# Attention keys and latent queries in DRAM, by head and then row

## The chip, the cores and the metric

The kernel runs on one core of one Trainium2 chip. The metric is device time in microseconds of one execution. A core has TensorE (PE; its weight loads are listed as PEld), VectorE (DVE), ScalarE (ACT), GpSimd (POOL) and SyncE (SP), and 16 DMA engines. Every DMA of this kernel is issued by SyncE, in the order of its one instruction stream.

## What is computed

Two network blocks of two layers each, batch 1, 512 tokens, width 1024, all in float32. The first block mixes sliding-window attention, retention and gated linear attention. The second block also carries 256 context tokens; its even layer has windowed attention and a latent attention of 8 heads, its odd layer grouped and differential attention. Cut to the part in which the change lies, the even layer is:

```
qa, ka, va, cq, ckv, kpe = split_cols(t @ w_in, EVEN_SIZES)
qb  = rms_norm_2(cq, q_norm) @ w_uq           # 8 heads x (64 + 32)
kvb = rms_norm_2(ckv, kv_norm) @ w_ukv        # 8 heads x (64 keys + 64 values)
qb  = [qb[..., :64], rope(qb[..., 64:])]
kb  = [kvb[..., :64], rope(kpe)]
kb_all = concatenate([kb_context, kb])        # 256 + 512 keys
ob  = softmax(qb @ kb_all.T / sqrt(96)) @ vb_all
```

## The kernel before

Activations lie with features on the 128 partitions and tokens along the row. Products are kept near float32 by splitting each operand into a high and a low part and making three products: weights come into `wr`, ScalarE rounds them to `wh`, GpSimd or VectorE makes the rest `wl` (`weights`, L417 to L422, L398, L400). Three `wr` buffers and two of `wh` and `wl` take turns.

Queries, keys and values of each attention are projected first, written to scratch in DRAM (`put`, L816), and read back head by head (`get`, L819). A projected tile has 128 partitions: two heads of 64 rows, or four heads of 32 rows where a rotation handles the two halves of a head apart. The tiles wait in `rp`, nine buffers of the work pool that many steps share; a buffer is free again when its put has landed.

The scratch tensors of keys are `rk` and `ak` (first block), `eka` (even, windowed), `ekn` (even, latent), `okc` and `okd` (odd layer). Each is laid out as [high or low, 64 rows, heads, tokens]. The latent queries without position, `qn` (in DRAM `eqnc` for the context and `eqnm` for the 512 tokens), are laid out as [128, 8 heads, tokens]: rows 0 to 63 high parts, rows 64 to 127 low parts. So in a put of two heads the destination steps over heads first and over rows second, and the two steps can't be joined.

`even_project` makes three generators: `window` (keys, queries and values of the windowed part), `latent`, and the scratch. `latent` normalizes the key latent, then per pair of heads makes one product, splits it into two `rp` tiles and puts both into `ekn` (8 puts); values go to `evb` in 8 puts (4 for the context); the shared rotated key to `ekp`; then the query latent, four products of two heads each and 8 puts into `qn`; then the rotated queries to `qp`. `weave` interleaves generators in proportion to the numbers given to it, and the tile scheduler sets each engine's order from priorities. For the 256 context tokens `latent` is woven into the first steps of the first block's second layer; for the 512 tokens it is woven into `even_window`, the windowed attention, whose blocks it shares PSUM, `rp` and SyncE's queue with. `even_latent` then reads per head `ekn` (four gets of 64 rows), `qn`, `qp` (two gets) and `evb`.

Of the kernel before, what the change touches and what calls it, by code (L numbers as in the profile page):

```python
# [12 lines left out]
F32R = mybir.dt.float32r  # L13
# [11 lines left out]
S = 512  # L25
# [3 lines left out]
TK = S + CL  # L29
# [170 lines left out]
class Net:  # L200
# [627 lines left out]
    def k_put(self, scr, pieces, h0, c0, T, n=4):  # L828

        for xi, parts in enumerate(pieces):  # L830
            for hl, t in enumerate(parts):
                dst = scr[hl, xi * 32:xi * 32 + 32, h0:h0 + n, c0:c0 + T]
                self.put(dst.rearrange("r h t -> h r t"), t)

    def k_put_both(self, scr, parts, c0, T):
        for hl, t in enumerate(parts):
            for xi in range(2):
                dst = scr[hl, xi * 32:xi * 32 + 32, 0:2, c0:c0 + T]
                self.put(dst.rearrange("r h t -> h r t"), t[xi * 64:xi * 64 + 64])

    def k_get(self, at, scr, h, c0, T):

        out = []
        for hl in range(2):
            t = at("k", [128, T], F32R)
            for d in range(2):
                self.get(t[d * 64:d * 64 + 64], scr[hl, :, h, c0:c0 + T])
            out.append(t)
        return out

# [392 lines left out]
    def layer1(self, l, h, ready):  # L1243

        nc, I = self.nc, self.I

        def fm(i):
            return ready.pop(i) if i in ready else self.dense(I["w_in"][l, i].rearrange("p k c -> p (k c)"), h, S, tag="d")

        ob = self.oy1(S)  # L1250
        og, orr = [ob[:, 2], ob[:, 3]], [ob[:, 0], ob[:, 1]]
        rq, rk = self.scr([128, 4, S], f"rq{l}"), self.scr([2, 64, 4, S], f"rk{l}")
        aq, ak = self.scr([128, 8, S], f"aq{l}"), self.scr([2, 64, 2, S], f"ak{l}")
        rv, av = self.scr([128, NT, 4, 128], f"rv{l}"), self.scr([128, NT, 2, 128], f"av{l}")
        gates = self.scr([128, KD, S], f"gate{l}")

        def values(v, n, dst):
            hl = self.rp([128, n, 2, 64], F32R)
            src = v.rearrange("p (h d) -> p h d", d=64)
            self.split_ps(src, hl[:, :, 0, :], hl[:, :, 1, :])  # L1260
            self.put(dst, hl.rearrange("p h a d -> p h (a d)"))

        def project1():
            tab = self.load_angles(self.rtab)
            self.q_put(rq, self.rope(partial(fm, 2), partial(fm, 3), tab, S), 0)
            yield
            self.k_put(rk, self.rope(partial(fm, 4), partial(fm, 5), tab, S), 0, 0, S)
            yield
            for t, v in enumerate(self.dense_tok(I["w_tok_b"][l], h, S, 384, 2)):
                values(v[:, 0:256], 4, rv[:, t])  # L1270
                values(v[:, 256:384], 2, av[:, t])
            yield

        late = 2

        def project2():
            tab = self.load_angles(self.atab)
            self.k_put_both(ak, self.rope_both(fm(6), tab, S), 0, S)
            yield
            for g in range(2):  # L1280
                self.q_put(aq, self.rope(partial(fm, 7 + 2 * g), partial(fm, 8 + 2 * g), tab, S, 0.125), 4 * g)
                yield
            yield from gate_units(range(done, 8 - late))

        def gate_units(units):
            for i in units:
                self.put(gates[:, (6, 7, 4, 5, 0, 1, 2, 3)[i], :], self.silu2(fm(11 + i), S))
                yield

        q, k = (self.tl(self.c1, [128, S], F32, "q", 2) for _ in range(2))  # L1290
        nc.scalar.activation(q, fm(0), AF.Copy, scale=32 ** -0.5)
        yield
        nc.scalar.copy(k, fm(1))
        yield
        p1 = project1()
        done = len(ready)
        self.steps(gate_units(range(done)))
        gv, ga = [], []
        for v in self.dense_tok(I["w_tok_a"][l], h, S, 272, 3):
            gv.append(self.vsplit(v[:, 0:256], 4))  # L1300
            t = self.sm([128, 16])
            nc.scalar.copy(t, v[:, 256:272])
            ga.append(t)
        if l == 0:
            self.setup1()
        gt = self.bank([16, S])
        for t in range(NT):
            nc.tensor.transpose(gt[:, t * 128:t * 128 + 128], ga[t], self.ident)
        gaT = self.pg([16, S])
        nc.scalar.copy(gaT, gt)  # L1310
        yield
        with self.phase("gla") as ph:
            at = self.area(ph, "r", k=2, q=2, v=1)
            self.weave((self.gla(q, k, gv, gaT, l, og, ph), (31.2, 26)[l], 0),
                       (self.chain(p1, self.woven((project2(), (6.6, 24.2)[l], (-200, 0)[l]), (self.retention(at, rq, rk, rv, orr), 16, (300, 45)[l]))), 30, (30, 0)[l]))
        self.headnorm(og, self.gla_gain[:, l:l + 1])
        self.headnorm(orr)
        self.steps(gate_units(range(8 - late, 8)))
        oa = self.oy1(S)
        h = self.new_h(S)  # L1320

        def gated(ks):
            for k in ks:
                g = self.rp([128, S])
                nc.sync.dma_start(g, gates[:, k, :])
                src = oa[:, k, :] if k < 4 else ob[:, k - 4, :]
                nc.vector.scalar_tensor_tensor(src, src, 0.5, g, op0=ALU.mult, op1=ALU.mult)
                self.split(src, h[0][:, k, :], h[1][:, k, :], 1.0, "dve" if k in [1, 3, 5, 7] else "pool")

        gated((6, 7, 4, 5))  # L1330
        y = self.open_y()
        self.stage(low=3)
        with self.phase("win") as ph:
            at = self.area(ph, "w", k=4, q=6, v=2, p=10)
            self.weave((self.window1(at, aq, ak, av, self.sink1[:, l * 8:l * 8 + 8], oa), (26.4, 8)[l], 0),
                       (self.out_head(I["w_out"][l], h, S, y, range(4, 8)), (8, 5.6)[l], 0))
        gated(range(4))
        return h, y, range(4, 8)
# [48 lines left out]
    def setup2(self):  # L1387
        nc, I = self.nc, self.I
        self.cp = self.common
        t = self.pg([128, 384])  # L1390
# [16 lines left out]
        self.lam = self.cp.tile([128, 1], F32, name="lam")  # L1407
        nc.vector.tensor_sub(self.lam, sm[:, 0:1], sm[:, 1:2])
        nc.vector.tensor_scalar(self.lam, self.lam, LAM_INIT, None, op0=ALU.add)
        self.eka = self.scr([2, 64, 2, TK], "eka")  # L1410
        self.eva = self.scr([128, TK // 128, 2, 128], "eva")
        self.ekn = self.scr([2, 64, 8, TK], "ekn")
        self.ekp = self.scr([2, 32, TK], "ekp")
        self.evb = self.scr([128, TK // 128, 8, 128], "evb")
        self.okc = self.scr([2, 64, 2, TK], "okc")
        self.okd = self.scr([2, 64, 8, TK], "okd")
        self.ovc = self.scr([128, TK // 128, 2, 128], "ovc")
        self.ovd = self.scr([128, TK // 128, 2, 4, 128], "ovd")

# [31 lines left out]
    def even_project(self, h, T, c0, rope, pool):  # L1451

        nc, I = self.nc, self.I
        tag = "m" if rope else "c"
        W = I["ev_w_in"]
        fm = lambda i: self.dense(W[i].rearrange("p k c -> p (k c)"), h, T, tag="d")
        sc = dict(q=self.scr([128, 8, T], "eq" + tag), qn=self.scr([128, 8, T], "eqn" + tag),
                  qp=self.scr([64, 8, T], "eqp" + tag))

        def window():  # L1460
# [9 lines left out]
        def latent():  # L1470
# [3 lines left out]
            for i in range(4):  # L1474
                w = slice(i * 128, i * 128 + 128)
                ps = self.three(self.bank([128, T], "d"), [(hi[:, w], lo[:, w])], [ck])
                parts = self.rp([128, T], F32R), self.rp([128, T])
                self.split_ps(ps, *parts)
                for hl, p in enumerate(parts):
                    self.put(self.ekn[hl, :, 2 * i:2 * i + 2, c0:c0 + T].rearrange("r h t -> h r t"), p)  # L1480
            yield
            for t in range(T // 128):
                tok = slice(t * 128, t * 128 + 128)
# [29 lines left out]
            def up(hi, lo, i):  # L1513
                w = [slice(i * 256 + k * 128, i * 256 + k * 128 + 128) for k in range(2)]
                return self.three(self.bank([128, T], "d"), [(hi[:, s], lo[:, s]) for s in w], cq)
# [3 lines left out]
            for i in range(4):  # L1519
                parts = self.rp([128, T], F32R), self.rp([128, T])  # L1520
                self.split_ps(up(*w, i), *parts, sb)
                for hl, p in enumerate(parts):
                    self.put(sc["qn"][hl * 64:hl * 64 + 64, 2 * i:2 * i + 2, :].rearrange("r h t -> h r t"), p)
            yield
            w = self.weights(src[:, 1024:], 512)
            self.q_put(sc["qp"], self.rope(partial(up, *w, 0), partial(up, *w, 1), tab, T, sb), 0, 8, 16)
# [67 lines left out]
    def even_latent(self, at, sc, T, K, o):  # L1594
# [7 lines left out]

        def block(hd):
            kh, kl = self.k_get(at, self.ekn, hd, 0, K)
            qn = self.q_get(at, sc["qn"], hd, T)
            qp = at("q", [128, T], F32R)
            for d in range(2):
                self.get(qp[d * 64:d * 64 + 64], sc["qp"][:, hd, :])
            v = at("v", [128, K // 128, 128], F32R)
# [398 lines left out]
```

## Time and profile before

| | us |
|---|---|
| median of 3 runs (lowest, highest) | 2809.75 (2808.07, 2816.77) |
| the profiled execution, its time | 2816.5 |
| its span, first to last instruction | 2814.7 |

The profile is of one execution; the time of that execution is 1.8 us above its span. The mean granted TensorE clock over the span is 0.916 of full speed. The span is one chain of stages on one core; what a stage waits for is read from the rows of that stage. In rows in order of time a bracket gives the idle time of the engine before the instruction and what ended it. Times in the rows are us from the start of the span.

### The profile page before, as it was taken

The numbers are of one execution on the slowest core, as the hardware profiler recorded it, in microseconds if no ns is written. First come the engines' busy times: TensorE is split into PE (matmuls) and PEld (weight loads), VectorE is DVE, ScalarE is ACT, GpSimd is POOL, SyncE is SP. The second block draws the span as 40 slices with busy tenths as digits, with TensorE's granted clock in tenths as the row PEclk, the third lists the DMA queues.
The fourth block names the chain that finished last, engine by engine and source line by source line (L and its number), as shares of the span: only waits on it lengthen the run. The fifth ranks groups of instructions, "written<-read, shape, count | busy, mean of one in ns | idle before, by whom it ended". The sixth has DMA issues, their size and how long they took to land. (4 is left out here: it accounts for less than half of the span.)

```text
span 2814.7 us, 35280 instructions
## 1 busy us (share of the span) xinstructions
PE 2440.7 (87%) x12956; PEld 1984.9 (71%) x12956; DVE 1260.6 (45%) x2101; ACT 1178.0 (42%) x2219; POOL 1060.7 (38%) x754
## 2 busy tenths in 40 slices
PE   6978887778878886568999899999988989799997
PEld 4766666566666665447998887777776777688886
DVE  3655356244646644355452631222555777421212
ACT  3434364343537634346554532222344656332222
POOL 2435234334533541113444732323552222443334
PEclk9988898888979987779999999999988999899998
DMA  7364553335334553325653545454344353333332
GB/s 244 117 209 158 181 183 137 119 130 174 116 109 139 194 193 119 119 97 143 185 159 134 181 141 172 150 172 137 126 155 155 102 162 104 115 100 97 94 97 75
DMA packets 170816, 400.56 MB, mean 142 GB/s; under 512 B 19378, under 2 KB 60820, under 8 KB 167316
## 3 DMA queue, kind: packets, MB, share of 16 engines
q1 hardware_dynamic: 170644, 398.31, 43.3%
q8 instruction: 103, 1.69, 0.2%
q14 instruction: 69, 0.57, 0.1%
HBM read 339.85 MB, written 58.39 MB: 141 GB/s over the span
## 5 line engine op out<-in xcount | busy, mean ns | idle before, releaser
L398 POOL TENSOR_TENSOR wl<-wr,wh 128x1024 fp32r<-128x1024 f32 (+3 forms) x245 | 537.7, 2196 | 889.4 <-ACT wh L422 463.9
L422 ACT CAST wh<-wr 128x1024 fp32r<-128x1024 f32 (+3 forms) x367 | 353.9, 964 | 706.3 <-PE d L389 277.8
L389 PE MATMUL d<-hh,wh 128*128 128x512 f32 x960 | 398.7, 415 | 19.2 <-ACT hh L556 7.8
L389 PE MATMUL d<-hl,wh 128*128 128x512 f32 x960 | 393.4, 410 | 0.9 <-DVE hl L557 0.9
L389 PE MATMUL d<-hh,wl 128*128 128x512 f32 x960 | 261.4, 401 | 0.0
L400 DVE SCALAR_TENSOR_TENSOR wl<-wr,wh 128x1024 fp32r<-128x1024 f32 (+3 forms) x122 | 147.6, 1210 | 230.9 <-PE d L389 97.1
L389 PEld LDWEIGHTS d<-hh,wh 128*128 128x128 f32 x960 | 190.3, 198 | 61.3 <-ACT hh L556 8.4
L389 PEld LDWEIGHTS d<-hl,wh 128*128 128x128 f32 x960 | 189.8, 198 | 40.2 <-issue 2.9
L389 PEld LDWEIGHTS d<-hh,wl 128*128 128x128 f32 x960 | 184.3, 193 | 39.9 <-issue 1.6
L389 PE MATMUL b<-hh,wh 128*128 128x512 f32 x416 | 164.8, 396 | 0.0
L389 PE MATMUL b<-hl,wh 128*128 128x512 f32 x416 | 163.6, 393 | 0.0
L400 DVE SCALAR_TENSOR_TENSOR pg<-b,pg 128x512 fp32r<-128x512 f32 (+1 forms) x208 | 137.5, 667 | 54.9 <-ACT pg L404 50.4
L404 ACT CAST pg<-b 128x512 fp32r<-128x512 f32 (+1 forms) x208 | 117.5, 573 | 63.6 <-PE b L909 52.9
L882 DVE TENSOR_REDUCE sm<-s 128x1 f32<-128x768 f32 (+3 forms) x144 | 120.8, 847 | 30.8 <-PE s L389 29.8
L389 PE MATMUL d<-hc,wh 128*128 128x256 f32 x656 | 107.6, 315 | 22.5 <-DVE rp L400 11.4
L963 DVE SCALAR_TENSOR_TENSOR rp<-rp,d 128x512 f32<-128x512 f32 (+1 forms) x77 | 46.8, 608 | 167.8 <-ACT rp L962 167.6
L389 PE MATMUL d<-hid,wh 128*128 128x512 f32 (+1 forms) x528 | 115.6, 363 | 1.7 <-POOL hid L398 1.5
L1770 DVE SCALAR_TENSOR_TENSOR rp<-rp,b 128x512 f32<-128x512 f32 (+1 forms) x64 | 38.1, 595 | 175.0 <-PE b L389 174.3
L389 PEld LDWEIGHTS d<-hc,wh 128*128 128x128 f32 x656 | 97.3, 217 | 26.5 <-ACT wh L422 11.7
L389 PE MATMUL b<-hid,wh 128*128 128x512 f32 (+1 forms) x528 | 112.4, 361 | 0.0
L389 PE MATMUL b<-hh,wl 128*128 128x512 f32 x416 | 104.2, 390 | 0.0
L389 PEld LDWEIGHTS d<-hid,wh 128*128 128x128 f32 x528 | 90.7, 192 | 17.3 <-POOL hid L398 2.7
(419 smaller groups left out, 5062.6 us busy)
## 6 DMA issues: line engine op xcount, KB each, us to landing
wr<-in_ffn_w_in SPq DMA_DIRECT2D x132, 512.0 KB
mr<-in_ada_w SPq DMA_DIRECT2D x96, 512.0 KB
wr<-in_ffn_w_out SPq DMA_DIRECT2D x48, 512.0 KB
x<-x SPq DMA_DIRECT2D x20, 1024.0 KB
wr<-in_w_in SPq DMA_DIRECT2D x38, 512.0 KB
mr<-in_w_mod SPq DMA_DIRECT2D x32, 512.0 KB
wr<-in_ev_w_in SPq DMA_DIRECT2D x20, 512.0 KB
wr<-in_ffn_w_out SPq DMA_DIRECT2D x24, 384.0 KB
```

The costliest lines, as they stand in the source:

```text
L389: self.nc.tensor.matmul(out, lhsT, rhs, start=start, stop=stop)
L398: self.nc.gpsimd.tensor_sub(out, src, hi)
L400: self.nc.vector.scalar_tensor_tensor(out, src, scale, hi, op0=ALU.mult, op1=ALU.subtract)
L404: self.nc.scalar.copy(hi, src)
L422: nc.scalar.copy(hi[:, :n], raw[:, :n])
L882: nc.vector.reduce_max(c, s, axis=AX.X, negate=True)
L963: nc.vector.scalar_tensor_tensor(t, t, 1.0, ps, op0=ALU.add, op1=ALU.mult)
L1770: nc.vector.scalar_tensor_tensor(g, g, 0.5, pu, op0=ALU.mult, op1=ALU.mult)
```

## The change

The key scratch tensors get the layout [high or low, heads, 64 rows, tokens], and `qn` becomes [2, 8 heads, 64 rows, tokens]. `k_put`, `k_put_both` and `k_get` index accordingly. The puts of `ekn` and `qn` name their destination as one run of 128 rows, two heads of 64. A head's `qn` now lies in two places, high and low, so that its read becomes two gets of 64 rows.

```
--- before.py
+++ after.py
@@ -829,14 +829,12 @@
 
         for xi, parts in enumerate(pieces):
             for hl, t in enumerate(parts):
-                dst = scr[hl, xi * 32:xi * 32 + 32, h0:h0 + n, c0:c0 + T]
-                self.put(dst.rearrange("r h t -> h r t"), t)
+                self.put(scr[hl, h0:h0 + n, xi * 32:xi * 32 + 32, c0:c0 + T], t)
 
     def k_put_both(self, scr, parts, c0, T):
         for hl, t in enumerate(parts):
             for xi in range(2):
-                dst = scr[hl, xi * 32:xi * 32 + 32, 0:2, c0:c0 + T]
-                self.put(dst.rearrange("r h t -> h r t"), t[xi * 64:xi * 64 + 64])
+                self.put(scr[hl, 0:2, xi * 32:xi * 32 + 32, c0:c0 + T], t[xi * 64:xi * 64 + 64])
 
     def k_get(self, at, scr, h, c0, T):
 
@@ -844,7 +842,7 @@
         for hl in range(2):
             t = at("k", [128, T], F32R)
             for d in range(2):
-                self.get(t[d * 64:d * 64 + 64], scr[hl, :, h, c0:c0 + T])
+                self.get(t[d * 64:d * 64 + 64], scr[hl, h, :, c0:c0 + T])
             out.append(t)
         return out
 
@@ -1249,8 +1247,8 @@
 
         ob = self.oy1(S)
         og, orr = [ob[:, 2], ob[:, 3]], [ob[:, 0], ob[:, 1]]
-        rq, rk = self.scr([128, 4, S], f"rq{l}"), self.scr([2, 64, 4, S], f"rk{l}")
-        aq, ak = self.scr([128, 8, S], f"aq{l}"), self.scr([2, 64, 2, S], f"ak{l}")
+        rq, rk = self.scr([128, 4, S], f"rq{l}"), self.scr([2, 4, 64, S], f"rk{l}")
+        aq, ak = self.scr([128, 8, S], f"aq{l}"), self.scr([2, 2, 64, S], f"ak{l}")
         rv, av = self.scr([128, NT, 4, 128], f"rv{l}"), self.scr([128, NT, 2, 128], f"av{l}")
         gates = self.scr([128, KD, S], f"gate{l}")
 
@@ -1407,13 +1405,13 @@
         self.lam = self.cp.tile([128, 1], F32, name="lam")
         nc.vector.tensor_sub(self.lam, sm[:, 0:1], sm[:, 1:2])
         nc.vector.tensor_scalar(self.lam, self.lam, LAM_INIT, None, op0=ALU.add)
-        self.eka = self.scr([2, 64, 2, TK], "eka")
+        self.eka = self.scr([2, 2, 64, TK], "eka")
         self.eva = self.scr([128, TK // 128, 2, 128], "eva")
-        self.ekn = self.scr([2, 64, 8, TK], "ekn")
+        self.ekn = self.scr([2, 8, 64, TK], "ekn")
         self.ekp = self.scr([2, 32, TK], "ekp")
         self.evb = self.scr([128, TK // 128, 8, 128], "evb")
-        self.okc = self.scr([2, 64, 2, TK], "okc")
-        self.okd = self.scr([2, 64, 8, TK], "okd")
+        self.okc = self.scr([2, 2, 64, TK], "okc")
+        self.okd = self.scr([2, 8, 64, TK], "okd")
         self.ovc = self.scr([128, TK // 128, 2, 128], "ovc")
         self.ovd = self.scr([128, TK // 128, 2, 4, 128], "ovd")
 
@@ -1454,7 +1452,7 @@
         tag = "m" if rope else "c"
         W = I["ev_w_in"]
         fm = lambda i: self.dense(W[i].rearrange("p k c -> p (k c)"), h, T, tag="d")
-        sc = dict(q=self.scr([128, 8, T], "eq" + tag), qn=self.scr([128, 8, T], "eqn" + tag),
+        sc = dict(q=self.scr([128, 8, T], "eq" + tag), qn=self.scr([2, 8, 64, T], "eqn" + tag),
                   qp=self.scr([64, 8, T], "eqp" + tag))
 
         def window():
@@ -1477,7 +1475,7 @@
                 parts = self.rp([128, T], F32R), self.rp([128, T])
                 self.split_ps(ps, *parts)
                 for hl, p in enumerate(parts):
-                    self.put(self.ekn[hl, :, 2 * i:2 * i + 2, c0:c0 + T].rearrange("r h t -> h r t"), p)
+                    self.put(self.ekn[hl, 2 * i:2 * i + 2, :, c0:c0 + T].rearrange("h r t -> (h r) t"), p)
             yield
             for t in range(T // 128):
                 tok = slice(t * 128, t * 128 + 128)
@@ -1520,7 +1518,7 @@
                 parts = self.rp([128, T], F32R), self.rp([128, T])
                 self.split_ps(up(*w, i), *parts, sb)
                 for hl, p in enumerate(parts):
-                    self.put(sc["qn"][hl * 64:hl * 64 + 64, 2 * i:2 * i + 2, :].rearrange("r h t -> h r t"), p)
+                    self.put(sc["qn"][hl, 2 * i:2 * i + 2].rearrange("h r t -> (h r) t"), p)
             yield
             w = self.weights(src[:, 1024:], 512)
             self.q_put(sc["qp"], self.rope(partial(up, *w, 0), partial(up, *w, 1), tab, T, sb), 0, 8, 16)
@@ -1602,8 +1600,9 @@
 
         def block(hd):
             kh, kl = self.k_get(at, self.ekn, hd, 0, K)
-            qn = self.q_get(at, sc["qn"], hd, T)
-            qp = at("q", [128, T], F32R)
+            qn, qp = at("q", [128, T], F32R), at("q", [128, T], F32R)
+            for d in range(2):
+                self.get(qn[d * 64:d * 64 + 64], sc["qn"][d, hd])
             for d in range(2):
                 self.get(qp[d * 64:d * 64 + 64], sc["qp"][:, hd, :])
             v = at("v", [128, K // 128, 128], F32R)
```

The first place is SyncE's stream where the context's latent queries are put; `eqnc` is their DRAM tensor, `rp` the tiles in SBUF, `wr` a weight load. This is one piece of the difference.

```order
-L816 DMA eqnc<-rp_4588 2x64x256
-L816 DMA eqnc<-rp_4589 2x64x256
-L816 DMA eqnc<-rp_4601 2x64x256
-L816 DMA eqnc<-rp_4602 2x64x256
+L816 DMA eqnc<-rp_4588 128x256
+L816 DMA eqnc<-rp_4589 128x256
+L816 DMA eqnc<-rp_4601 128x256
+L816 DMA eqnc<-rp_4602 128x256
 L417 DMA wr_4758<-in_w_tok_a 128x544
```

The order is the same; the destination of each put reads 128 rows where it read two times 64.

The second place is the last two key puts of the 512 tokens and what SyncE issues behind them: queries of the window (`eq`), latent values (`evb`), and keys of the window's second group (`ek` from `eka`). Before:

```order
L816 DMA ekn<-rp_9538 2x64x512
L816 DMA ekn<-rp_9539 2x64x512
L819 DMA eq_9879<-eqm 128x512
L819 DMA eq_9881<-eqm 128x512
L819 DMA eq_9883<-eqm 128x512
L816 DMA evb<-rp_9665 128x512
L819 DMA ek_9871<-eka 64x768
L816 DMA evb<-rp_9669 128x512
L819 DMA ek_9871<-eka 64x768
L816 DMA evb<-rp_9677 128x512
L816 DMA evb<-rp_9681 128x512
L816 DMA evb<-rp_9689 128x512
```

And with the change:

```order
L816 DMA ekn<-rp_9546 128x512
L816 DMA ekn<-rp_9547 128x512
L819 DMA eq_9887<-eqm 128x512
L819 DMA eq_9889<-eqm 128x512
L819 DMA eq_9891<-eqm 128x512
L816 DMA evb<-rp_9673 128x512
L819 DMA ek_9879<-eka 64x768
L816 DMA evb<-rp_9677 128x512
L819 DMA ek_9879<-eka 64x768
L816 DMA evb<-rp_9685 128x512
L816 DMA evb<-rp_9689 128x512
L816 DMA evb<-rp_9697 128x512
```

No DMA has moved past another; the two puts changed their shape.

The third place is the reads of the first two heads of the 512 tokens in `even_latent`. Before:

```order
L819 DMA ek_10656<-ekn 64x768 x2
L819 DMA ek_10659<-ekn 64x768 x2
L819 DMA eq_10662<-eqnm 128x512
L819 DMA eq_10664<-eqpm 64x512 x2
L819 DMA ev_10667<-evb 128x6x128
L819 DMA ek_10713<-ekn 64x768 x2
L819 DMA ek_10716<-ekn 64x768 x2
L819 DMA eq_10719<-eqnm 128x512
L819 DMA eq_10721<-eqpm 64x512 x2
L819 DMA ev_10724<-evb 128x6x128
```

And with the change:

```order
L819 DMA ek_10664<-ekn 64x768 x2
L819 DMA ek_10667<-ekn 64x768 x2
L819 DMA eq_10670<-eqnm 64x512 x2
L819 DMA eq_10671<-eqpm 64x512 x2
L819 DMA ev_10676<-evb 128x6x128
L819 DMA ek_10722<-ekn 64x768 x2
L819 DMA ek_10725<-ekn 64x768 x2
L819 DMA eq_10728<-eqnm 64x512 x2
L819 DMA eq_10729<-eqpm 64x512 x2
L819 DMA ev_10734<-evb 128x6x128
```

Each head has one more get, the second half of `qn`, ahead of its `qp`. In the two loops of `even_latent` the 16 added gets shift some weight loads and value reads by a few places; elsewhere SyncE's order, and that of the other engines, is the one of before.

The 8 key puts and 8 query puts for the context and as many for the 512 tokens, 32 in all, are the only ones whose shape changes. The puts of `okd` and `rk` stay four heads of 32 rows, those of `ak`, `eka` and `okc` two heads of 32 rows; only the distance between heads and rows in DRAM is another. The key reads stay 64 rows, which now lie next to each other.

## Rows read from the trace of the kernel before

**Rows 1.** The page: the span, and TensorE with its share.

```profile
span 2814.7 us, 35280 instructions
...
PE 2440.7 (87%) x12956; PEld 1984.9 (71%) x12956; DVE 1260.6 (45%) x2101; ACT 1178.0 (42%) x2219; POOL 1060.7 (38%) x754
```

**Rows 2.** By tile, SyncE issues: ns min/median/max, first and last start us.

```profile
L819 SPq DMA_DIRECT2D ek<-ekn x32: 444/564/1392, 1248.2 to 1419.6; - x32
...
L816 SPq DMA_DIRECT2D ekn<-rp x16: 495/2688/5262, 516.0 to 1129.2; - x16
...
L816 SPq DMA_DIRECT2D eqnm<-rp x8: 485/4487/5209, 1198.8 to 1224.2; - x8
...
L816 SPq DMA_DIRECT2D gate<-rp x16: 319/358/1974, 87.9 to 826.7; - x16
```

**Rows 3.** Stretches: length, busy PE, PEld, DVE, ACT, POOL; PEclk, DMA share, GB/s.

```profile
519.00:548.00 29.00, 14.28 (x81) 12.89 (x79) 3.24 (x6) 6.94 (x13) 5.28 (x3) 0.80 0.35 121
575.00:596.00 21.00, 8.92 (x31) 6.04 (x30) 2.83 (x5) 5.12 (x12) 2.37 (x1) 0.59 0.60 212
1110.00:1134.00 24.00, 9.54 (x46) 6.51 (x44) 8.26 (x22) 8.32 (x22) 0.74 (x1) 0.72 0.13 52
1116.00:1153.00 37.00, 4.53 (x18) 2.71 (x18) 6.23 (x14) 5.41 (x13) 0.00 (x0) 0.56 0.34 123
1153.00:1160.00 7.00, 6.92 (x25) 5.27 (x25) 1.08 (x3) 1.46 (x4) 0.53 (x2) 0.65 0.54 160
1223.00:1249.00 26.00, 6.16 (x27) 2.68 (x26) 5.51 (x11) 5.84 (x15) 1.47 (x2) 0.50 0.43 147
```

**Rows 4.** In order of time, SyncE, 1085 to 1165 us: start, length, DMAs.

```profile
1104.02 30.46 SPq L816 DMA_DIRECT2D ekn<-rp  x8
...
1147.83 2.95 SPq L816 DMA_DIRECT2D evb<-rp  x5
```

**Rows 5.** Who waited for whom, 1085 to 1160 us: total, times, longest.

```profile
ACT rp L404 <- DMA ekn<-rp: 22.4, 6, 4.8
```

**Rows 6.** In order of time, TensorE; in brackets idle before, and releaser.

```profile
1123.09 1.22 PE L389 MATMUL d<-wh,lat 128*128 128x512 f32 x2 [3.71 <-DVE rp L400]
...
1129.22 0.66 PE L942 MATMUL b<-ident,pg 128*128 128x128 f32 x2 [4.49 <-DVE sm L894]
1152.61 0.55 PE L389 MATMUL s<-ek,eq 128*128 128x256 f32 x1 [22.73 <-DMA ek<-eka]
```

**Rows 7.** In order of time, SyncE then TensorE, 1198 to 1250 us.

```profile
1198.79 30.37 SPq L816 DMA_DIRECT2D eqnm<-rp  x8
...
1228.43 1.65 PE L389 MATMUL d<-pg,ev 128*128 128x512 f32 x2 [4.84 <-ACT pg L404]
1238.45 0.79 PE L389 MATMUL d<-pg,ev 128*128 128x512 f32 x1 [8.38 <-ACT pg L404]
...
1248.53 1.01 PE L389 MATMUL b<-mod_sel,ms 128*128 128x2 f32 x4 [6.57 <-ACT pg L944]
```

**Rows 8.** Who waited for whom, 1180 to 1270 us.

```profile
ACT rp L503 <- DMA eqnm<-rp: 13.5, 3, 4.8
...
ACT rp L406 <- DMA eqnm<-rp: 3.8, 1, 3.8
```

**Rows 9.** In order of time, SyncE, ScalarE and TensorE, 516 to 592 us.

```profile
517.16 17.07 SPq L816 DMA_DIRECT2D ekn<-rp  x7
...
546.32 1.04 ACT L422 CAST wh<-wr 128x1024 fp32r<-128x1024 f32 x1 [9.10 <-DMA wr<-in_ev_w_uq]
...
579.44 1.04 ACT L422 CAST wh<-wr 128x1024 fp32r<-128x1024 f32 x1 [8.75 <-DMA wr<-in_w_in]
...
548.01 1.01 PE L389 MATMUL b<-blk,rp 128*128 128x1 f32 x4 [9.14 <-ACT rp L503]
...
582.34 0.38 PE L1308 MATMUL b<-ident,sm 128*16 128x128 f32 x1 [7.02 <-ACT sm L1302]
...
589.91 0.38 PE L1308 MATMUL b<-ident,sm 128*16 128x128 f32 x1 [5.05 <-ACT sm L1302]
```

More of the change, by code (lines that the diff above doesn't have):

```diff
@@ L831, in k_put @@
             for hl, t in enumerate(parts):
-                dst = scr[hl, xi * 32:xi * 32 + 32, h0:h0 + n, c0:c0 + T]
-                self.put(dst.rearrange("r h t -> h r t"), t)
+                self.put(scr[hl, h0:h0 + n, xi * 32:xi * 32 + 32, c0:c0 + T], t)
     def k_put_both(self, scr, parts, c0, T):
@@ L837, in k_put_both @@
             for xi in range(2):
-                dst = scr[hl, xi * 32:xi * 32 + 32, 0:2, c0:c0 + T]
-                self.put(dst.rearrange("r h t -> h r t"), t[xi * 64:xi * 64 + 64])
+                self.put(scr[hl, 0:2, xi * 32:xi * 32 + 32, c0:c0 + T], t[xi * 64:xi * 64 + 64])
     def k_get(self, at, scr, h, c0, T):
@@ L846, in k_get @@
             for d in range(2):
-                self.get(t[d * 64:d * 64 + 64], scr[hl, :, h, c0:c0 + T])
+                self.get(t[d * 64:d * 64 + 64], scr[hl, h, :, c0:c0 + T])
             out.append(t)
@@ L1251, in layer1 @@
         og, orr = [ob[:, 2], ob[:, 3]], [ob[:, 0], ob[:, 1]]
-        rq, rk = self.scr([128, 4, S], f"rq{l}"), self.scr([2, 64, 4, S], f"rk{l}")
-        aq, ak = self.scr([128, 8, S], f"aq{l}"), self.scr([2, 64, 2, S], f"ak{l}")
+        rq, rk = self.scr([128, 4, S], f"rq{l}"), self.scr([2, 4, 64, S], f"rk{l}")
+        aq, ak = self.scr([128, 8, S], f"aq{l}"), self.scr([2, 2, 64, S], f"ak{l}")
         rv, av = self.scr([128, NT, 4, 128], f"rv{l}"), self.scr([128, NT, 2, 128], f"av{l}")
@@ L1409, in setup2 @@
         nc.vector.tensor_scalar(self.lam, self.lam, LAM_INIT, None, op0=ALU.add)
-        self.eka = self.scr([2, 64, 2, TK], "eka")
+        self.eka = self.scr([2, 2, 64, TK], "eka")
         self.eva = self.scr([128, TK // 128, 2, 128], "eva")
-        self.ekn = self.scr([2, 64, 8, TK], "ekn")
+        self.ekn = self.scr([2, 8, 64, TK], "ekn")
         self.ekp = self.scr([2, 32, TK], "ekp")
         self.evb = self.scr([128, TK // 128, 8, 128], "evb")
-        self.okc = self.scr([2, 64, 2, TK], "okc")
-        self.okd = self.scr([2, 64, 8, TK], "okd")
+        self.okc = self.scr([2, 2, 64, TK], "okc")
+        self.okd = self.scr([2, 8, 64, TK], "okd")
         self.ovc = self.scr([128, TK // 128, 2, 128], "ovc")
@@ L1456, in even_project @@
         fm = lambda i: self.dense(W[i].rearrange("p k c -> p (k c)"), h, T, tag="d")
-        sc = dict(q=self.scr([128, 8, T], "eq" + tag), qn=self.scr([128, 8, T], "eqn" + tag),
+        sc = dict(q=self.scr([128, 8, T], "eq" + tag), qn=self.scr([2, 8, 64, T], "eqn" + tag),
                   qp=self.scr([64, 8, T], "eqp" + tag))
@@ L1479, in latent @@
                 for hl, p in enumerate(parts):
-                    self.put(self.ekn[hl, :, 2 * i:2 * i + 2, c0:c0 + T].rearrange("r h t -> h r t"), p)
+                    self.put(self.ekn[hl, 2 * i:2 * i + 2, :, c0:c0 + T].rearrange("h r t -> (h r) t"), p)
             yield
@@ L1522, in latent @@
                 for hl, p in enumerate(parts):
-                    self.put(sc["qn"][hl * 64:hl * 64 + 64, 2 * i:2 * i + 2, :].rearrange("r h t -> h r t"), p)
+                    self.put(sc["qn"][hl, 2 * i:2 * i + 2].rearrange("h r t -> (h r) t"), p)
             yield
@@ L1604, in block @@
             kh, kl = self.k_get(at, self.ekn, hd, 0, K)
-            qn = self.q_get(at, sc["qn"], hd, T)
-            qp = at("q", [128, T], F32R)
+            qn, qp = at("q", [128, T], F32R), at("q", [128, T], F32R)
+            for d in range(2):
+                self.get(qn[d * 64:d * 64 + 64], sc["qn"][d, hd])
             for d in range(2):
```

## Prediction

> **What bounds the kernel now.** TensorE is busy 87% of the span [rows 1], so most stages are TensorE's, and a change that only moves DMA data is worth something only where TensorE stands still because of it. I therefore looked for the changed transfers first, by tile: what SyncE spends on issuing them. A put of 256 KB whose rows are one run (`gate<-rp`, 128 rows of 512) takes SyncE 358 ns in the median. The puts of `ekn` take 2688 ns in the median and up to 5262, those of `eqnm` 4487 and up to 5209, though the latter are as large as `gate<-rp` [rows 2]. An issue that long is not the instruction's own work; SyncE is held back by something that is full.
>
> The windows say what. While the 512 tokens' key puts run, from 1110 to 1134 us, the 16 DMA engines are busy 0.13 of the time, at 52 GB/s [rows 3]. 0.13 times 16 is 2.1 engines. The reader is to see a core with 14 idle DMA engines whose SyncE can't get rid of its puts: eight puts of 256 KB are 2.1 MB, and at 52 GB/s that is 40 us. In order of time this is just what happens: the eight puts begin at 1104.02, take SyncE 30.46 us to issue, and the run of value puts behind them starts only at 1147.83 [rows 4].
>
> The Trainium skill gives a reason ("DMA: Bandwidth & Descriptors", on why a DMA increments its semaphore by 16, the paragraph on how many engines): a DMA is spread over as many engines, up to 16, as divide the size of the slowest dimension of both sides. For a destination of two heads by 64 rows that is 2. The trace agrees with its 0.13.
>
> Who suffers: ScalarE waits 22.4 us in 6 waits for `rp` buffers that `ekn` puts still hold [rows 5], and its stream stands meanwhile, so that VectorE and then TensorE run dry. TensorE idles 3.71, 4.49 and at last 22.73 us, the last for `ek`, the window's keys of its second group, whose gets are behind those puts and the value puts in SyncE's stream [rows 6]. Over 1116 to 1153 it is busy 4.53 of 37 us, at a granted clock of 0.56; there is nothing else that fills the hole.
>
> The same shape comes three more times. The `eqnm` puts hold SyncE from 1198.79 for 30.37 us, and TensorE idles 4.84, 8.38 and 6.57 us [rows 7], behind ScalarE's 13.5 and 3.8 us of waiting for them [rows 8]. For the context the puts are half as long: `ekn` holds SyncE 17.07 us from 517.16, weight loads queue behind it, ScalarE waits 9.10 us for one, TensorE 9.14 for ScalarE; then `eqnc`, where ScalarE waits 8.75 us for a weight load and TensorE stands for 7.02 and 5.05 us [rows 9].
>
> **The change part by part.**
>
> The 32 puts of `ekn` and `qn` get 128 rows as their outer dimension on both sides. I price one like `gate<-rp`: 0.36 us of SyncE, and data on all engines. If 16 engines do what 2 did, 43.8 us (1104.02 to 1147.83) become 5.5 us for eight puts, less than the 6 or so us that producing the tiles takes; the hold is gone. Stretch by stretch:
>
> - 1116 to 1153. The last `ek` get has to wait for the value puts ahead of it, and these for splits that stood behind the held `rp` buffers. Without the hold I let the three idle stretches of 30.9 us [rows 6] shrink to one last wait of 4 us, the latency of the get and the rest of the splits: 27 us saved. Bounds: TensorE's idle time is 32.5 us; a quarter of it may come back, so 20 to 32.
> - 1223 to 1249. TensorE is idle 19.8 us [rows 7]. The four rotated query puts (`eqpm`, eight heads by 16 rows) keep their shape and still run there, so 3 us stay: 17 saved, 12 to 22 (above 19.8 since the work there runs at a clock of 0.50 [rows 3], the lower level of 1.2 GHz, and would mostly run at the upper).
> - 519 to 548. Idle 29.00 - 14.28 = 14.7 us [rows 3]; weight loads still have to land, so 13 saved, 7 to 17 with the clock of 0.80.
> - 575 to 596. Idle 21.00 - 8.92 = 12.1 us at a clock of 0.59. Three loads still have to come in a row after the puts: 9 saved, 4 to 15.
>
> Sum of the four: 66 us. What follows each stretch is TensorE's (1153 to 1160: 6.92 busy of 7.00 [rows 3]), so an earlier start is an earlier end.
>
> The clock comes back late after a stall: 0.65 in 1153 to 1160 though TensorE is full [rows 3]. At the upper level those 6.9 us would be 4.5. I don't add this, it is in the upper bounds.
>
> The reads of `qn` become two gets of 64 rows: 16 more DMAs. The trace has a get of 64 rows: `ek<-ekn`, 564 ns of SyncE [rows 2], so 9.0 us of SyncE in all. They lie in the two loops of `even_latent`, where a head's reads go out while TensorE works on the head before. On the path is the first head's only: 0.6 us per loop, 1 us in all. Lower bound 0, upper bound 9.0 if every one delays its head. The Trainium skill speaks against this part ("DMA: Bandwidth & Descriptors", rules for kernel authors: don't cut a transfer into partition halves, one of 128 partitions is better). By that rule alone the loss would be some part of the 9.0 us; I keep 1.
>
> The other layouts (`rk`, `ak`, `eka`, `okc`, `okd`): their puts keep two or four heads as outer dimension, so what holds them back stays; their gets and those of `ekn` read 64 rows that are now neighbours, with the same rows and bytes. I cost this at nothing; what hides it is that the reads of one head run under the work on another. A gain or loss of 2 us either way is in the range.
>
> 66 - 1 = 65 us less. The profiled execution took 2816.5 us (span 2814.7), so the sum gives 2751.5 for it; that execution was 6.75 us above the median of the three, 2809.75. In terms of the median: 2744.75, say **2745**.
>
> **The rivals.**
>
> *The holes close only in part.* Where the hold goes, the next thing in line may be nearly as late: at 1152.61 the get of `ek` also stands behind eight value puts, and in the context's stretch behind weight loads which need a free `wr` buffer. For it: TensorE is idle 13% of the time even away from here. Against: between the puts SyncE has nothing else to do for long, and DMA is nearly empty. If half of each lower bound were all that came (20 + 12 + 7 + 4 = 43, halved 22), the time is 2788; I let this case reach from 2772 to 2801.
>
> *Nothing changes.* It could be that two engines are used not because of the two heads, but because of the rows' distance in DRAM or of `rp` as the source; then 128 rows in one run fill the same two. For it: nothing in the rows names the cause. Against: `gate<-rp` comes from `rp` too, with 128 rows, and takes 358 ns. The time would be 2810 plus 1 for the gets, 2811.
>
> *Slower.* The two key reads per head and the two halves of `qn` now come out of one dense block each, and a dense block may be read slower than rows far apart; with the added gets each head of `even_latent` then starts late. It decides from the point where a head's reads outlast the work on the head before. The added gets alone are 9.0 us; if the puts gave nothing, that is 2819. For the reads to eat 65 us besides, each of 16 heads would have to start 3.5 us later. Against: before, `ek` reads cause no wait in the loop worth a row.
>
> *More than forecast.* All idle time of the four stretches, 32.5 + 19.8 + 14.7 + 12.1 = 79.1, goes, and the work left runs at full clock (2.0 + 3.1 + 2.9 + 3.7 = 11.7 by busy time and clock of rows 3): 91 us, 2719. That leaves nothing idle where elsewhere 13% is, so it is the low end.
>
> **How the numbers follow.** The forecast, with bounds 20 + 12 + 7 + 4 = 43 less 5 for gets (2772) and 91 (2719), has a chance of 0.82. Closing in part: 0.09. More than 91: 0.02. Nothing changes: 0.04. Slower: 0.03. The range 2719 to 2772 holds the first alone. A measurement of this kernel can tell about 0.3%, 8 us; faster by more than that is 0.82 + 0.09 + 0.02 = 0.93, within it 0.04, slower 0.03.
>
> **What would show it.** Right: the issue times of `ekn<-rp` and `eqnm<-rp` fall to some 0.4 us, no ScalarE wait is put down to them, the DMA share during the puts rises well above 0.13 for a few us, and the 22.73 us before the first `s<-ek` of the second group is below 6. Each stretch shrinks by its term. Wrong: the issue times stay in the thousands of ns (then the two engines have another cause); or they fall and TensorE waits as long for a weight load, a value put or the rotated queries' puts instead (then the next in line was as late); or TensorE's idle time between heads of `even_latent` grows by more than 1 us a head.

## The result and the profile after

The changed kernel takes 2735.53 us in the median of 4 runs (2719.65 to 2739.86); beside them the kernel before took 2812.23 (2808.07 to 2816.77). The ratio is 0.9721, 95% interval 0.9697 to 0.9744: 76.7 us less, where 65 were forecast. Timed a second time, it took 2728.46 beside 2810.79 (0.9707, 0.9685 to 0.9729), 82.3 us less. The profiled execution took 2731.66.

The page of the changed kernel answers to [rows 1].

```profile
span 2729.9 us, 35294 instructions
...
PE 2429.0 (89%) x12956; PEld 1976.1 (72%) x12956; DVE 1257.8 (46%) x2101; ACT 1177.8 (43%) x2219; POOL 1062.4 (39%) x754
```

TensorE's share rises by two points while its busy time falls by 11.7 us with the same 12956 matmuls: part of the gain is not idle time but the same work done in less time.

SyncE's issues by tile in the changed kernel answer to [rows 2].

```profile
L819 SPq DMA_DIRECT2D ek<-ekn x32: 444/587/1237, 1162.7 to 1336.6; - x32
...
L816 SPq DMA_DIRECT2D ekn<-rp x16: 319/353/446, 518.4 to 1075.8; - x16
...
L819 SPq DMA_DIRECT2D eq<-eqnm x16: 444/594/1280, 1167.4 to 1340.5; - x16
L816 SPq DMA_DIRECT2D eqnm<-rp x8: 319/320/327, 1129.8 to 1141.7; - x8
```

The slowest `ekn` put, 446 ns, is now quicker than the quickest was (495). No ScalarE wait is put down to `ekn` or `eqnm` puts any longer; the 22.4 us of [rows 5] and the 17.3 of [rows 8] are gone. The split gets of `qn` (`eq<-eqnm`) take 594 ns each; before, one get of 128 rows did the same.

In order of time, SyncE's stream of the changed kernel answers to [rows 4] and to the head of [rows 7].

```profile
1070.36 5.78 SPq L816 DMA_DIRECT2D ekn<-rp  x8
...
1083.12 3.54 SPq L816 DMA_DIRECT2D evb<-rp  x5
...
1129.84 12.17 SPq L816 DMA_DIRECT2D eqnm<-rp  x8
```

The eight key puts take 5.78 us from the first to the last, not 30.46, and the run of five value puts starts 12.8 us after the first of them, not 43.8. Before, the first two of the eight took 0.53 and 0.49 us to issue and each of the last five 4.6 to 5.3. At 52 GB/s a put of 256 KB takes 5.0 us (an estimate from [rows 3]), so SyncE got rid of them only as fast as they were carried. Of the 12.17 us of the query puts the eight issues are 2.6; between them SyncE waits for nothing that is full, but for the next tile.

The four stretches are now compared between the same matmuls. TensorE runs 12956 in both traces in nearly the same order, so that a stretch can be found again by counting: from number 2166 to 2328 (context keys), 2361 to 2500 (context queries), 4637 to 4767 (keys), 4971 to 5129 (queries), and 5130 to 5250, the start of `even_latent`. The windows of the kernel before, columns as in [rows 3]:

```profile
510.20:560.50 50.30, 32.69 (x164) 26.73 (x162) 8.88 (x19) 14.76 (x30) 12.66 (x10) 0.83 0.30 99
565.10:605.20 40.10, 27.67 (x142) 22.83 (x141) 12.88 (x24) 13.09 (x27) 9.12 (x6) 0.74 0.41 140
1105.10:1165.10 60.00, 26.84 (x131) 20.72 (x131) 20.45 (x46) 16.80 (x40) 2.27 (x4) 0.69 0.30 103
1205.10:1257.10 52.00, 29.66 (x160) 21.10 (x159) 24.43 (x53) 21.15 (x47) 9.43 (x8) 0.70 0.34 115
1257.20:1292.00 34.80, 23.04 (x123) 17.64 (x123) 21.56 (x41) 19.55 (x42) 6.42 (x8) 0.90 0.40 106
```

The same five in the changed kernel, and ahead of them the 6 us of its key puts:

```profile
1071.00:1077.00 6.00, 5.91 (x36) 4.93 (x36) 5.64 (x14) 3.64 (x10) 0.40 (x1) 1.00 0.88 328
...
511.30:545.40 34.10, 28.17 (x163) 22.73 (x161) 8.91 (x19) 14.32 (x30) 12.74 (x10) 0.95 0.48 159
550.10:572.90 22.80, 22.80 (x141) 19.23 (x141) 13.71 (x24) 13.06 (x27) 9.20 (x6) 1.00 0.57 189
1071.40:1095.80 24.40, 23.40 (x131) 18.56 (x131) 19.97 (x47) 16.47 (x40) 3.05 (x4) 1.00 0.72 250
1136.20:1169.20 33.00, 28.13 (x161) 20.50 (x159) 24.42 (x53) 20.94 (x47) 9.91 (x8) 0.90 0.53 158
1169.20:1208.40 39.20, 27.18 (x123) 21.05 (x122) 21.94 (x41) 19.75 (x42) 6.41 (x8) 0.80 0.39 101
```

While the key puts run, the DMA engines are busy 0.88 of the time at 328 GB/s, where they were busy 0.13 at 52. The four stretches shrink by 16.2, 17.3, 35.6 and 19.0 us, 88.1 together. Length less busy PE, TensorE's idle time in them, falls from 17.6 + 12.4 + 33.2 + 22.3 = 85.5 to 5.9 + 0 + 1.0 + 4.9 = 11.8, by 73.7. The other 14.4 us are the busy time, 116.9 before and 102.5 after: the same matmuls at granted clocks of 0.90 to 1.00, not 0.69 to 0.83. The fifth stretch takes 4.4 us longer, at a clock of 0.80 for 0.90. 88.1 less 4.4 is 83.7, of the 84.8 us between the two spans.

### The profile page after: what moved, and what is told of

The parts are those of the page before. It is cut to its first block, busy times and chain, and to the rows that moved or that the text cites. A ratio compares the mean times of both kernels' runs of the same rounds, so it can differ in the third digit from the quotient of the medians.

```text
span 2729.9 us, 35294 instructions
## 1 busy us (share of the span) xinstructions
PE 2429.0 (89%) x12956; PEld 1976.1 (72%) x12956; DVE 1257.8 (46%) x2101; ACT 1177.8 (43%) x2219; POOL 1062.4 (39%) x754
## 5 line engine op out<-in xcount | busy, mean ns | idle before, releaser
L400 DVE SCALAR_TENSOR_TENSOR wl<-wr,wh 128x1024 fp32r<-128x1024 f32 (+3 forms) x122 | 146.2, 1198 | 226.2 <-PE d L389 98.0
L389 PEld LDWEIGHTS d<-hh,wl 128*128 128x128 f32 x960 | 184.3, 194 | 39.4 <-issue 1.2
L880 DVE TENSOR_REDUCE sm<-s 128x1 f32<-128x768 f32 (+3 forms) x144 | 120.8, 847 | 31.9 <-PE s L389 31.1
L389 PE MATMUL d<-hc,wh 128*128 128x256 f32 x656 | 102.7, 306 | 20.0 <-ACT wh L422 11.7
L483 POOL TENSOR_TENSOR sm<-sm,mhalf 128x4 f32<-128x4 f32 (+3 forms) x33 | 45.8, 1388 | 149.6 <-DVE sm L481 140.1
```

What stands on the lines that cost most here:

```text
L389: self.nc.tensor.matmul(out, lhsT, rhs, start=start, stop=stop)
L400: self.nc.vector.scalar_tensor_tensor(out, src, scale, hi, op0=ALU.mult, op1=ALU.subtract)
L483: nc.gpsimd.tensor_tensor(r, ms, self.mhalf[:, None, :].to_broadcast([128, nt, n]), op=ALU.pow)
L880: nc.vector.reduce_max(c, s, axis=AX.X, negate=True)
```

## The experiments

Theory: a put whose destination steps over two heads first is carried by two DMA engines; this holds SyncE, which holds `rp`, ScalarE and TensorE, in four places that don't depend on each other. Rivals: the two engines come from the layout as such (rows far apart), or the gain comes from the reads of denser blocks.

**Dense heads that can't be joined** (of the changed kernel). Behind each head's 64 rows lie 8 unused ones, so the layout and its reads stay and only the two heads no longer make one run.

```
-        self.ekn = self.scr([2, 8, 64, TK], "ekn")
+        self.ekn = self.scr([2, 8, 72, TK], "ekn")
...
-                    self.put(self.ekn[hl, 2 * i:2 * i + 2, :, c0:c0 + T].rearrange("h r t -> (h r) t"), p)
+                    self.put(self.ekn[hl, 2 * i:2 * i + 2, 0:64, c0:c0 + T], p)
```

(`qn` likewise; the gets read the 64 used rows.) Expected:

> The changed kernel with eight unused rows behind the 64 rows of each head of ekn and qn. The layout stays head by head with neighbouring rows and the reads stay as changed; only two heads no longer join into one run, so the 32 puts are two heads by 64 rows again. Theory (the outer dimension of two confines a put to two engines): the issue times are back near 2.7 us median for ekn with a DMA share of 0.13 in the stretch, and the time is that of the kernel before plus some 4 us for the added gets, 2808 to 2822. Rival (it is the neighbouring rows in DRAM that make the puts fast): 2730 to 2745.

Measured: 2818.8 us (10 runs) beside 2808.86 (13 runs), ratio 1.003, 1.0015 to 1.0044. Its issues by tile, and the window of [rows 3] in which its key puts run:

```profile
L816 SPq DMA_DIRECT2D ekn<-rp x16: 493/2683/5249, 512.6 to 1125.1; - x16
...
L816 SPq DMA_DIRECT2D eqnm<-rp x8: 483/4512/5194, 1194.9 to 1220.4; - x8
```

```profile
1110.00:1134.00 24.00, 5.43 (x24) 3.17 (x22) 5.59 (x15) 5.39 (x16) 0.00 (x0) 0.68 0.13 52
```

The whole gain is gone, with the same 0.13 and 52 GB/s as before. The dense layout and its reads are worth nothing by themselves. The 0.3% above the kernel before can be theirs or that of the 16 added gets, which this kernel has too.

**Old layout, one put for each head** (of the kernel before). Each put of two heads is cut into two of one head, 64 rows each; layouts and reads stay as they were.

```
-                    self.put(self.ekn[hl, :, 2 * i:2 * i + 2, c0:c0 + T].rearrange("r h t -> h r t"), p)
+                    for j in range(2):
+                        self.put(self.ekn[hl, :, 2 * i + j, c0:c0 + T], p[j * 64:j * 64 + 64])
```

(`qn` likewise.) Expected:

> The kernel before, layout and reads untouched, with each of the 32 puts cut into two of one head, 64 rows far apart in DRAM. Theory: 64 rows spread over the engines, no issue above 1.5 us, and the gain is there without the change of layout and without added gets: 2728 to 2748; SyncE pays 32 more issues of some 0.5 us, beside other work. Rival (one run in DRAM is needed): 2800 to 2820.

Measured: 2737.53 us (2731.01 to 2741.72), ratio 0.9731, 0.971 to 0.9752. Its issues by tile, and the window of its key puts:

```profile
L816 SPq DMA_DIRECT2D ekn<-rp x32: 495/566/1416, 510.4 to 1075.8; - x32
...
L816 SPq DMA_DIRECT2D eqnm<-rp x16: 445/568/1094, 1126.3 to 1140.2; - x16
```

```profile
1067.00:1077.00 10.00, 9.81 (x56) 7.49 (x55) 8.03 (x19) 6.79 (x18) 1.13 (x2) 1.00 0.89 196
```

A gain as large as the change's, with no layout changed. What counts is that the put's outer step is over many rows. Rows that lie far apart in DRAM are no hindrance. The Trainium skill ("DMA: Bandwidth & Descriptors", why a DMA increments its semaphore by 16) says that the slowest dimension sets how many engines carry a DMA, the largest number up to 16 that divides it on both sides. By that rule two heads outside give 2, and 64 rows give 16. Both runs agree, by a share of 0.13 and one of 0.89. The traces' records of single transfers say it more directly: in the kernel before, from 1110 to 1134 us, two transfers are under way for 0.88 of the time and three for the rest, never fewer; with a gap between the heads it is two for 0.85 and three for the rest; with one put a head, from 1067 to 1077 us, it is 14 or more for 0.78. The Trainium skill (same page, rules for kernel authors) calls it useless to cut a transfer into two halves of the partitions; here the halves saved 71 us, since the uncut put had two heads outside.

**The keys alone, and the queries alone.** The first is the changed kernel with `qn` as before; the second is the kernel before with only `qn` changed, as in the change's diff. Of the first:

```
-                    self.put(sc["qn"][hl, 2 * i:2 * i + 2].rearrange("h r t -> (h r) t"), p)
+                    self.put(sc["qn"][hl * 64:hl * 64 + 64, 2 * i:2 * i + 2, :].rearrange("r h t -> h r t"), p)
...
-            for d in range(2):
-                self.get(qn[d * 64:d * 64 + 64], sc["qn"][d, hd])
+            qn = self.q_get(at, sc["qn"], hd, T)
```

> The changed kernel with qn as before (layout, puts of two heads, one get of 128 rows). Theory: the two ekn stretches keep their gain (16 us near 520 to 548 and 36 us near 1116 to 1153 in the traces), the two qn stretches lose theirs (17 and 19 us), and the 4 to 5 us lost at the start of the latent attention are not paid: 2754 to 2768, 50 us under before. Rival (the stretches aren't independent: what one gives is taken back by the next hold): under 40 us in all.

> The kernel before with only qn changed (layout, puts of one run, two gets). Theory: 17 and 19 us gained, 4 to 5 lost: 2774 to 2788, some 31 us under before, and with the run of keys alone the two gains sum to that of the whole change within 6 us. Rival (the stretches aren't independent): the sum of the two differs from the whole by more than 12 us.

Measured: keys alone 2756.05 us, ratio 0.979 (0.9759 to 0.9822); queries alone 2779.4, ratio 0.9881 (0.9852 to 0.9911). Issues by tile, keys alone and then queries alone:

```profile
L816 SPq DMA_DIRECT2D ekn<-rp x16: 319/368/447, 519.1 to 1092.1; - x16
...
L816 SPq DMA_DIRECT2D eqnm<-rp x8: 483/4488/5256, 1146.3 to 1171.7; - x8
```

```profile
L816 SPq DMA_DIRECT2D ekn<-rp x16: 496/2656/5270, 505.8 to 1097.8; - x16
...
L816 SPq DMA_DIRECT2D eqnm<-rp x8: 319/320/326, 1167.4 to 1179.3; - x8
```

Beside 2808.86 these are 52.8 and 29.5 us, 82.3 together: the whole of the change. Each edit acts in its own stretches alone. Lengths in us between the same matmuls, one trace each:

| stretch | before | changed | can't be joined | one put a head | keys alone | queries alone |
|---|---|---|---|---|---|---|
| context keys | 50.3 | 34.1 | 52.5 | 38.0 | 32.5 | 50.3 |
| context queries | 40.1 | 22.8 | 39.4 | 28.6 | 39.3 | 22.8 |
| keys | 60.0 | 24.4 | 59.7 | 26.1 | 24.3 | 60.2 |
| queries | 52.0 | 33.0 | 53.0 | 31.8 | 52.2 | 31.9 |
| start of `even_latent` | 34.8 | 39.2 | 38.5 | 41.0 | 38.0 | 42.1 |

In the context's queries a joined put is better than two of one head: over all traces of this document the stretch takes 22.8 to 23.9 us in the five with joined puts there and 28.6 to 31.6 in the four with a put for each head. The context's keys point the same way, 31.5 to 35.2 us in eight traces against 38.0 in one. For the 512 tokens the two kinds differ by less than 2 us.

**The added gets.** The last line of the table is the surprise: all five other kernels are slower there than the first trace of the kernel before, two of them (one put a head, keys alone) with its single get of `qn`. Three runs bear on it: the kernel before with only the get split; the changed kernel with `qn` as [8 heads, 128, tokens], read by one get and put head by head; and the kernel before once more.

```
-            qn = self.q_get(at, sc["qn"], hd, T)
...
+            for d in range(2):
+                self.get(qn[d * 64:d * 64 + 64], sc["qn"][d * 64:d * 64 + 64, hd, :])
```

```
-                    self.put(sc["qn"][hl, 2 * i:2 * i + 2].rearrange("h r t -> (h r) t"), p)
+                    for j in range(2):
+                        self.put(sc["qn"][2 * i + j, hl * 64:hl * 64 + 64], p[j * 64:j * 64 + 64])
...
-            for d in range(2):
-                self.get(qn[d * 64:d * 64 + 64], sc["qn"][d, hd])
+            self.get(qn, sc["qn"][hd])
```

> The kernel before, its layouts and puts untouched; only the latent queries of a head are read as two gets of 64 rows instead of one of 128. Theory 1 (the added gets are what costs 4 to 8 us at the start of the latent attention): that stretch takes 4 to 8 us longer than the 55.5 us of the kernel before in every profile, and the time is 2813 to 2817 beside 2809. Theory 2 (the stretch is longer because TensorE's granted clock stays low in it, and the gets lie under other work): no more than 1 us from the gets, time 2808 to 2811, and the stretch is long or short with its granted clock.

> The changed kernel, but the latent queries are laid out by head and then all 128 rows (high and low parts together), so a head is read in one get of 128 rows; its puts are then one head and 64 rows each, 16 instead of 8. Theory 1 (added gets cost 4 to 8 us): 2727 to 2731, under the 2735.5 of the changed kernel by that. Theory 2 (gets hidden): 2733 to 2738, no difference that can be told. The issue time of a put should be about 0.5 us in both, as in the run with one put for each head.

> The kernel before once more, for a second trace of the start of its latent attention. Where the first trace has 34.8 us at a granted clock of 0.90 from TensorE's 5130th to its 5250th matmul, every other kernel has 38.0 to 42.4 us at 0.74 to 0.80, with one get of latent queries or two. If the clock alone decides and rises early or late by chance, this trace may show either, and 38 us or more would put the loss to chance; if the layout or the gets cost it, it shows 34.8 us again.

Measured: split get alone 2814.25 us beside 2812.03, ratio 1.0014 (0.9997 to 1.0031); one get kept 2730.36, ratio 0.9726 (0.9698 to 0.9754); the kernel before once more, a single run, 2804.01. By their times alone the first two lie in the ranges that were expected if the gets cost 4 to 8 us. But the kernel before stood at 2812.03 beside them, 3 us above the 2809 on which the first range rests; and one get kept has head-by-head puts too, which lengthen its context queries (30.2 us for 22.8), so that its time doesn't price the gets. The stretch itself tells more. The start of `even_latent` in the three, in this order:

```profile
1257.10:1296.00 38.90, 27.62 (x121) 21.20 (x122) 21.84 (x41) 19.73 (x42) 6.41 (x8) 0.76 0.36 95
```

```profile
1162.80:1205.20 42.40, 29.17 (x122) 22.64 (x123) 21.91 (x41) 19.82 (x42) 6.41 (x8) 0.74 0.42 99
```

```profile
1244.80:1282.50 37.70, 27.09 (x122) 21.06 (x122) 21.86 (x41) 19.70 (x42) 6.42 (x8) 0.77 0.37 98
```

With one get kept the stretch is no shorter than with two, and the kernel before, run again, needs 37.7 us and not 34.8, with the busy PE and the clock of the others. So 34.8 was an execution with a higher clock (0.90). What remains goes with the queries' stretch ahead: the five traces in which that has its old length need 34.8 to 38.9 us here, the nine in which it is short need 38.7 to 42.4, by means 37.6 and 40.8. Some 3 us are lost there again, then, by one get or by two. The traces show a wait that goes with it. Who waited for what around the first head, in the changed kernel, with one put a head (who waited for `eqnm`; a single get), and in the kernel before:

```profile
PE s L389 <- DMA eq<-eqnm: 2.1, 1, 2.1
```

```profile
  PE s L389: 3.4, 1
```

```profile
PE s L389 <- DMA eq<-eqpm: 0.6, 1, 0.6
```

In each of the nine traces TensorE waits 1.0 to 3.5 us for the first head's `qn`; in the five it waits 0.6 to 1.3 us at this place, and not for that get. TensorE reaches the first head earlier than its reads are there. How much of the 3 us is this wait and how much the clock is not shown.

The split gets may cost anything up to 8.7 us by the interval, nothing too; from matmul 5250 to 7000, which holds the rest of the latent attention, all kernels need 248.5 to 250.0 us.

**The puts that still have two or four heads outside.** The rotated keys (`k_put_both`, two heads by 32 rows) put head by head; then also the rotated queries of four heads by 32 rows, with `qn` by one get.

```
-                self.put(scr[hl, 0:2, xi * 32:xi * 32 + 32, c0:c0 + T], t[xi * 64:xi * 64 + 64])
+                for h in range(2):
+                    self.put(scr[hl, h, xi * 32:xi * 32 + 32, c0:c0 + T], t[xi * 64 + h * 32:xi * 64 + h * 32 + 32])
```

```
+                if n == 4:
+                    for h in range(n):
+                        self.put(scr[o:o + r, h0 + h, :], t[h * r:h * r + r])
+                    continue
                 self.put(scr[o:o + r, h0:h0 + n, :].rearrange("r h t -> h r t"), t)
```

> The changed kernel with the rotated keys of two heads by 32 rows (the layers' own keys, the even layers' and the odd layer's) put head by head, 32 rows each, twice as many puts. If every put with two heads as outer dimension holds SyncE back where other puts stand behind it, the 3.7 to 5 us of TensorE's waiting between 1015 and 1050 us get shorter: 2 to 8 us less than the 2735.5 of the changed kernel. If these puts (0.55 us of SyncE in the median) are too few in a row to hold it back, the time stays at 2733 to 2738, or rises by the 20 added issues of half a microsecond, 10 us at the very most.

> The two kernels before this one together, and besides them the rotated queries of four heads by 32 rows put head by head. By the same reckoning 4 to 12 us less than the 2735.5 of the changed kernel if four heads as outer dimension hold SyncE back too (their puts go up to 1.86 us of issue between 1003 and 1024 us); no difference, or a loss of some us for the added issues, if they don't.

Measured: rotated keys cut 2726.72 us, ratio 0.9699 (0.9675 to 0.9723); all cut 2738.41, ratio 0.9745 (0.9718 to 0.9771). The first is 9 us under the 2735.53 of the changed kernel, a little more than the 2 to 8 expected, but the two were not timed side by side. So the changed kernel, this one, and this one with `qn` by one get were timed together.

> The changed kernel once more, to stand beside the next two on one chip: 2731 to 2740.

> The changed kernel with the rotated keys put head by head, as before (2726.7 then). If those 9 us under the changed kernel are its own, it is again 5 to 12 us under the changed kernel in this call; if they were the chip's, the two agree within 3 us. In the profile the gain should lie where these puts stand (the context at 575 to 596, and 1015 to 1050 us).

> The changed kernel with both edits: rotated keys put head by head, and latent queries laid out by head and then 128 rows, so one get reads a head. If the two gains (9 and 5 us) are real and lie in different places, 2720 to 2725; if one of them was chance, 2725 to 2733; if both, 2733 to 2740.

Measured: 2728.46 (2721.45 to 2731.66; 2731 to 2740 was expected), 2724.08 (2720.09 to 2727.52) and 2730.84 (2723.11 to 2731.49). The first two ratios are 0.9707 (0.9685 to 0.9729) and 0.9694 (0.9673 to 0.9716): 4.4 us, well inside the intervals, so it can't be told whether the rotated keys cut beat the changed kernel. Both together show no gain (0.9713, 0.9691 to 0.9734). In the run with all cut the 16 issues of `aq`, 0.54 us in the median before, are 64:

```profile
L816 SPq DMA_DIRECT2D aq<-rp x64: 302/420/1414, 231.0 to 696.5; - x64
```

A tile of four heads costs four times 0.42 us of SyncE instead of 0.54, and this kernel was the slowest of the three timed together that have the whole gain (2738.41 beside 2730.36 and 2726.72). Where puts didn't queue up behind each other, a small outer step cost little, and no gain from cutting it can be told.

## Why the prediction was right

- **The cause**: two heads outside mean two engines, and SyncE is held. Shown: a gap between heads brings the 0.13 and the 2.7 us issues back, and one head a put removes them without any layout. The rival in which the distance of the rows is the cause is refuted by the second of these, and the one in which dense blocks are read slower has no support: from matmul 5250 to 7000, with the rest of the latent attention in it, TensorE takes 248.6 us before and 249.8 after, and for the heads of the context (matmul 3642 to 3944) 62.1 and 64.1, where that rival needed 65 us more. What stays open is the 0.3% of the kernel with the gap.
- **1116 to 1153**, 27 us forecast (20 to 32): 35.6 measured, above its bound. A last wait of 4 us was left standing for the `ek` get, and idle time in the whole stretch is now 1.0 us. The clock of 0.69 became 1.00, 3.4 us of the gain by the busy time. The 43.8 us to the run of value puts became 12.8, not the 5.5 set down for them, since gets and two single value puts lie between; TensorE waits for none of it.
- **1223 to 1249**, 17 us (12 to 22): 19.0.
- **519 to 548**, 13 us (7 to 17): 16.2, of which 4.5 is busy time.
- **575 to 596**, 9 us (4 to 15): 17.3, above its bound. The three weight loads that were to come in a row cause no idle time at all (0.0 us of 22.80), and 4.9 us are the clock, 0.74 to 1.00.
- **The sum**: 88.1 for 66. The step that was mis-sized is the price of a stretch: the sum has idle time alone, 66 us where 73.7 went (13 us were kept, 3 of them in 575 to 596, where none is left; the stretches between the matmuls are a little wider than the forecast's, 85.5 us idle for 79.1), and leaves the clock, 14.4 us measured, to the upper bounds. The second pair of traces agrees: the four stretches shrink by 15.1, 16.1, 34.6 and 17.8, 83.6 us, of which 73.5 are idle time.
- **The range**: all four terms were too small, two of them beyond their own bounds, and 88.1 is nearer to the 91 us of *More than forecast* than to 66. The mechanism is the one that was forecast; the time lies well inside the range because the range reaches down to that rival's sum.
- **The gets**, 1 us: the 4.4 us lost between the first two traces was mostly not theirs. The second pair loses 1.0 there. What the sum had at 0.6 us a loop, the first head's read, is a wait of 2.1 and 1.0 us in the two traces of the changed kernel.
- **The other layouts at nothing**: no run shows a gain or a loss of theirs.

The medians, 76.7 and 82.3 us, are less than 88.1 would give. 4.4 of it is the fifth stretch. The rest is in which executions were profiled: that of the kernel before lies 4.3 us above its median and that of the changed kernel 3.9 below, so that the spans differ by 84.8. Single executions of one kernel differ by as much: the two traces of the kernel before are 12.5 us apart, 5.5 of it ahead of the first stretch. In the second pair the spans differ by 72.3 only, since 9.8 us are lost between matmul 2500 and 4637, from the second stretch to the third. All 14 traces scatter there from 491.8 to 503.7 us, and the kernel before alone has 499.9 and 493.9.

## What to carry to other kernels

Look for DMA issues that take microseconds on the issuing engine while the DMA engines are nearly idle, and then at the outermost step of the access: a 2 there was the fault here, and a merge of the steps or one DMA for each head cured it, so take whichever the layout permits. It paid only where such transfers stood in a row and a buffer or a read waited behind them. When a stall is priced, add the busy time on both sides of it that ran at the lower clock.

## What was unexpected of the hardware

- A put of 128 rows in one run takes SyncE 0.32 us (`eqnm`, changed kernel), one of 64 rows 0.57 (`eqnm`, one put a head), one of 32 rows 0.42 (`aq`, all cut): two halves cost 3.6 times the issue of the whole.
- During the key puts the engines were equally busy with joined puts (0.88) and with two of 64 rows (0.89), but moved 328 GB/s and 196; the windows hold other transfers too, so the cause is not shown.
- TensorE's granted clock after a stall differs from one execution of the same kernel to the next: 0.90 and 0.77 over the same 120 matmuls, in a stretch of 34.8 and 37.7 us.
